# A two-part transformer kernel on one core: stacked attention scores, gathering that begins earlier, fewer chunks made ahead, and three changes of order

## The chip, the core and the metric

The kernel runs on one core of a Trainium2 chip. The metric is the device time of one execution in microseconds (us). TensorE does the matrix products, VectorE and ScalarE elementwise work, GpSimd and SyncE issue the transfers (GpSimd those that gather rows by index), and 16 DMA engines move the data. In the profile these are PE, DVE, ACT, POOL and SP; PEld is TensorE's loading of weights.

## The reference

All is float32, on 256 tokens of width 1024 and 256 context tokens. First come two layers of mix and PEER, then two layers of hybrid mixer and memory attention (not shown but for the hybrid's forget gates), then a norm.

```python
for l in range(2):                                   # first block
    f, p, q, k, v, gates = split_proj(h @ w_in[l])   # h: normed tokens; the context likewise
    q, k = rope(rmsnorm(q)), rope(rmsnorm(k))        # 8 query heads, 2 key heads of 64
    ya = attend(q, [k, k_ctx], [v, v_ctx]) @ attn_proj[l]     # 512 keys; context alone: 256
    x = x + gate * ((gates * [fourier(f), pool(p), ya]).sum() @ w_out[l])
    # PEER: 16384 experts, 8 heads, 16 experts per head and token
    q = (h2 @ wq).reshape(C, 8, 2, 128)
    s = einsum('chpd,hpnd->chpn', q, sub_keys)       # 128 keys in each of two halves
    s1, i1 = top_k(s[:, :, 0], 16); s2, i2 = top_k(s[:, :, 1], 16)
    top, pos = top_k(s1[..., None] + s2[..., None, :], 16)    # 16 of the 256 sums
    g = softmax(top)
    a = gelu(einsum('chkd,cd->chk', u_tab[eidx], h2))         # 128 experts per token
    x = x + gate * einsum('chk,chkd->cd', g * a, v_tab[eidx])
# second block, hybrid mixer: among its parts
log_f = log_sigmoid(f_b + b_forget)                  # forget gates, 8 heads
```

Layer 0 does PEER for tokens and context (512 rows), layer 1 for the 256 tokens alone.

## The kernel before

**Products in three passes.** A float32 product is made of a high and a low half: `split` writes the high half (L128, a cast on ScalarE, `whi` for weights) and the rest (L129, a subtraction on VectorE, `wlo`), and `mm3` makes three products of them (L186, L187, L188; at L824 a variant of it). Weights come through `wload` into five raw buffers and four split ones. A product with unsplit operands, such as that of L645, takes TensorE two records in the trace.

**Mix.** The projections, the attention units and the gates of a layer are woven together. `qk_unit` makes normed and rotated queries and keys and transposes them (L634) into `qT` and `kT`; `attn1_unit` makes the scores of two heads (L645), the softmax, its transposition (L652) and the product with `v` (L660). Layer 0 has eight such units on 512 keys and eight on 256 (the context), layer 1 eight on 512.

**PEER.** All 16384 experts lie in 128 chunks of 128. For a part of the tokens (the dense ones, 320 of 512 in layer 0 and 192 of 256 in layer 1) every chunk is computed: `expert_in` takes the chunk of `peer_uT` times the tokens and a gelu to `G`, `A` is `G` times a table of routing weights (`win`, read back from device memory, `wd`, eight chunks at a time, L788), is split to `Ahl`, and the `Ahl` products (L186 to L188 and L824) add the chunk of `peer_v` to sums kept in PSUM. The other 192 or 64 tokens are gathered (`gathered`): for each of them one transfer fetches the rows of its 128 experts from `peer_uv`, 8 KB each (`gat`, L893, four buffers); VectorE makes the dot products with them (L896) and adds the weighted second halves to `gacc` (L910). GpSimd issues the gathers, and each needs `idx`, which the last step of the routing writes (L993).

**What is made ahead.** While VectorE does the routing, TensorE makes the first chunks' `G`: `AHEAD`, 13 in layer 0 and 30 in layer 1. In layer 1 all 30 are whole (`WHOLE`, L851): unsplit weights, full-precision products; all others are split (three passes; at L859 and L860 in layer 1). The main loop over 128 chunks then starts. It makes a chunk's missing `G`, its `A` and `Ahl`, and asks for gathers by the rule quoted here, so that they are spread over the loop from chunk 5 on:

```python
while gat and done < min(max(c - 5, 0) * ng // 119, ng):
```

**Order.** The Tile framework's scheduler orders the instructions of each engine from the order of the code, the priorities and its own model; each engine runs its list in order. `ng` is the number of gathers, 192 or 64. In the hybrid, the forget gates (`wfd` weights, loaded and split on the spot, `fdT`, L1262) come first, before the gates and the conv units, whose weights are prefetched.

Of the kernel before, what the change touches and what calls it, by code (L numbers as in the profile page):

```python
# [35 lines left out]
AHEAD = 13, 30  # L36
WHOLE = 0, 30
# [11 lines left out]
class Net:  # L49
# [370 lines left out]
    def rope(self, out, src, cos, sin, nh, nb, f, pool):  # L420
# [11 lines left out]
        nc.vector.tensor_add(out, out, t[:, :w])  # L432
# [50 lines left out]
    def mix(self, l, both):  # L483
# [3 lines left out]
        with ExitStack() as es:  # L487
# [4 lines left out]
            oT = [ap.tile([128, 4, TB], FR, name=n) for n in ("oTh", "oTl")]  # L492
# [4 lines left out]
            qT = bp.tile([128, 4, TB], F32, name="qT")  # L497
            kT = self.k_padded(bp, "kT", T)
# [115 lines left out]
    def qk_unit(self, tp, rope, ps, t, gi, out, v):  # L614

        nc = self.nc
        cg, sg, kg = rope
        nh = 2 if gi else 8
        s = slice(t * 128, t * 128 + 128)
        q = self.headnorm(ps[:, :nh * 64], nh, tp)  # L620
        r = tp.tile([128, 512], F32, tag="qr", name="qr", bufs=3)[:, :nh * 64]
        if t < 2:
            self.rope(r, q, cg[:, gi, t], sg[:, gi, t], nh, 2, 16, tp)
        else:
            nc.vector.tensor_tensor(r3(r, nh), r3(q, nh), bc(kg[:, gi, None, :], [128, nh, 64]), op=OP.mult)
        if gi:
            self.evac(v[:, t], ps[:, 128:256])
        yield True
        if gi:
            self.k_put(out, r, tp, s)  # L630
            return
        pt = self.psum(True)
        for j in range(4):
            nc.tensor.transpose(pt[:, j * 128:(j + 1) * 128], r[:, j * 128:(j + 1) * 128], self.ident)  # L634
        self.evac(out[:, :, s], r3(pt, 4))

    def attn1_unit(self, tp, qT, kT, v, oT, st, j, qt):
# [6 lines left out]
        for hh in range(2):  # L644
            nc.tensor.matmul(ps[hh][:, :nk], qT[:, j, q0:q0 + 128], kT[:, hh, g, k0:k0 + nk], start=True, stop=True)  # L645
# [52 lines left out]
    def peer(self, l, both):  # L698
# [9 lines left out]
        with ExitStack() as es:  # L708
# [22 lines left out]
            with ExitStack() as e2:  # L731
                np_ = self.pool(e2, "wqp", side="right")
                scs, made = {}, []
                for cg in range(5):
                    qT = np_.tile([128, 4, 512], F32, tag="pq", name="pq", bufs=2) if cg < 4 else None
                    for c in range(4 if cg < 4 else 1):
                        if cg < 4:
                            ps = self.psum(c % 2)
                            self.proj_T(ps[:, :T], hT, i["wq"][l, cg * 4 + c], 0, T)
                            nc.scalar.copy(qT[:, c, :T], ps[:, :T])  # L740
                        if c == 0 and cg:
                            for t in range(NT):
                                ps = self.psum()
                                for k in range(4):
                                    nc.tensor.matmul(ps[:, k * 128:k * 128 + 128], pq[:, k, t * 128:t * 128 + 128], keys[:, k],
                                                     start=True, stop=True)
                                sc = scs[cg - 1, t] = np_.tile([128, 512], F32, tag="score", name="score", bufs=8)
                                nc.scalar.copy(sc, ps)
                    pq = qT
                    if cg < 4:  # L750
                        keys = np_.tile([128, 4, 128], F32, tag="keys", name="keys", bufs=2)
                        nc.gpsimd.dma_start(keys, i["keysT"][l, cg])
                    if cg:
                        for t in range(NT):
                            sc = scs[cg - 1, t]
                            for c in range(4):
                                n = (cg - 1) * 4 + c
                                self.top16(np_, sc[:, c * 128:c * 128 + 128], v16[t][:, n], i16[t][:, n], "tk")
# [915 lines left out]
```

## Time and profile before

| what | value |
|---|---|
| median of 3 runs | 3415.68 us (3409.3 to 3416.18) |
| profiled execution, its time | 3411.22 us |
| its span on the chip | 3409.4 us |
| TensorE, VectorE, ScalarE, GpSimd busy | 95%, 76%, 51%, 15% |
| mean granted clock of TensorE | 0.979 |
| moved by DMA | 860.52 MB, mean 252 GB/s |

The span is the time between the first and the last instruction of one execution; its own time is 1.8 us longer. The stages by time in the span: mix of layer 0 to 470 us, its PEER to 1740 (the routing ends near 784), mix of layer 1 to 1990, its PEER to 2757 (the routing ends near 2175), then the two layers of the second block to 3080 and 3409.4. Matrix products are pipelined: the distance from one start to the next, not a single duration, is what one costs. A granted clock of 1 is 2.4 GHz, 0.5 is 1.2 GHz.

### The profile page before, as it was taken

Reading aid. Unit: us, or ns where it says so; the run is one execution under the profiler, and the core shown is the slowest. Engines: PE = TensorE matmul, PEld = TensorE weight load, DVE = VectorE, ACT = ScalarE, POOL = GpSimd, SP = SyncE. Lnnn points to the kernel's source line nnn. Section 1 sums busy time; section 2 is a strip of 40 time slices with the busy share of each in tenths; the row PEclk is TensorE's granted clock in tenths of the full one; section 3 lists DMA queues with packets and bytes.
Section 4 is the critical chain, followed back from the end, with each engine's and each line's share of the span. In section 5 each row is a group of like instructions: output and inputs, shape, how many; then the busy total and the mean of one; then the engine's idle time right before and its main releaser. Section 6 shows DMA issues by size and latency. Waiting matters only on the chain.

```text
span 3409.4 us, 53017 instructions
## 1 busy us (share of the span) xinstructions
PE 3247.6 (95%) x19425; PEld 2779.9 (82%) x19425; DVE 2598.9 (76%) x5429; ACT 1734.0 (51%) x3711; POOL 515.9 (15%) x436
## 2 busy tenths in 40 slices
PE   8999999889999999999999998889999989999998
PEld 5666788768888888888877997769999989889887
DVE  3533449997989888999966678589999967755875
ACT  3443333385444444444444544557777745555554
POOL 0000000112333333333300000122222100000000
PEclk9999999889999999999999998999999999999999
DMA  6556232568999999999945555789999844255433
GB/s 244 193 194 219 88 128 80 173 177 312 377 398 379 378 381 372 379 392 389 390 158 173 166 178 170 267 340 389 372 370 377 346 159 161 93 189 174 142 120 109
DMA packets 196453, 860.52 MB, mean 252 GB/s; under 512 B 23920, under 2 KB 25664, under 8 KB 159712
## 3 DMA queue, kind: packets, MB, share of 16 engines
q1 hardware_dynamic: 141840, 505.94, 41.4%
q0 software_dynamic: 54352, 351.20, 26.8%
q8 instruction: 153, 2.51, 0.3%
q14 instruction: 108, 0.88, 0.1%
HBM read 816.15 MB, written 40.89 MB: 251 GB/s over the span
## 4 chain that ended last, share of the span: by engine, by line
PE 46%; issue 27%; DVE 12%; DMA 8%; POOL 6%; ACT 1%; POOLq 0%; DVEq 0%; SPq 0%; ACTq 0%
PE pf L188 5%; PE pf L186 5%; PE pf L187 5%; PE pf L860 4%; POOL gat L893 4%; PE ps L188 4%; PE ps L187 4%; PE ps L186 4%; DMA gat<-peer_uv,idx 4%; DVE wlo L129 3%; PE ps L824 3%; DVE gacc L910 2%; PE pf L859 2%; PE pf L370 1%; DMA wd<-wb 1%
## 5 line engine op out<-in xcount | busy, mean ns | idle before, releaser
L129 DVE TENSOR_TENSOR wlo<-raw,whi 128x1024 fp32r<-128x1024 f32 x778 | 940.1, 1219 | 388.2 <-ACT whi L128 378.2
L128 ACT CAST whi<-raw 128x1024 fp32r<-128x1024 f32 x778 | 814.4, 1047 | 572.8 <-PE pf L187 193.9
L893 POOL DMA_INDIRECT gat<-peer_uv,idx x256 | 406.2, 1587 | 917.3 <-DVE gacc L910 886.4
L188 PE MATMUL pf<-h2hl,wlo 128*128 128x320 f32 (+2 forms) x1152 | 368.6, 320 | 42.6 <-DVE wlo L129 42.5
L186 PE MATMUL pf<-h2hl,whi 128*128 128x320 f32 (+2 forms) x1152 | 367.2, 319 | 0.4 <-ACT mo L321 0.3
L187 PE MATMUL pf<-h2hl,whi 128*128 128x320 f32 (+2 forms) x1152 | 366.5, 318 | 0.0
L896 DVE SCALAR_TENSOR_TENSOR gat<-gat,h 128x1024 f32<-128x1024 f32 x256 | 311.5, 1217 | 70.2 <-DMA gat<-peer_uv,idx 69.8
L910 DVE SCALAR_TENSOR_TENSOR gacc<-gat,pga,gacc 128x1024 f32<-128x1024 f32 x253 | 322.9, 1276 | 0.0
L187 PE MATMUL ps<-wlo,Ahl 128*128 128x512 f32 x768 | 302.5, 394 | 6.2 <-DVE wlo L129 6.2
L186 PE MATMUL ps<-whi,Ahl 128*128 128x512 f32 x768 | 301.0, 396 | 4.1 <-ACT Ahl L128 4.1
L188 PE MATMUL ps<-whi,Ahl 128*128 128x512 f32 x768 | 301.6, 393 | 0.5 <-DVE Ahl L129 0.5
L188 PEld LDWEIGHTS pf<-h2hl,wlo 128*128 128x128 f32 x1152 | 221.9, 193 | 52.3 <-DVE wlo L129 49.6
L860 PE MATMUL pf<-h2hl,whi 128*128 128x384 f32 x784 | 238.5, 360 | 3.8 <-ACT whi L128 3.6
L186 PEld LDWEIGHTS pf<-h2hl,whi 128*128 128x128 f32 x1152 | 221.3, 192 | 8.1 <-ACT mo L321 0.5
L187 PEld LDWEIGHTS pf<-h2hl,whi 128*128 128x128 f32 x1152 | 221.4, 192 | 7.3
L128 ACT CAST Ahl<-A 128x320 fp32r<-128x320 f32 (+1 forms) x256 | 103.7, 405 | 218.1 <-DVE A L791 213.5
L859 PE MATMUL pf<-h2hl,wlo 128*128 128x192 f32 x686 | 174.9, 255 | 0.0
L188 PEld LDWEIGHTS ps<-whi,Ahl 128*128 128x128 f32 x768 | 145.0, 189 | 33.6 <-DVE Ahl L129 1.0
L187 PEld LDWEIGHTS ps<-wlo,Ahl 128*128 128x128 f32 x768 | 144.9, 189 | 31.0 <-DVE wlo L129 8.7
L186 PEld LDWEIGHTS ps<-whi,Ahl 128*128 128x128 f32 x768 | 144.9, 189 | 27.9 <-ACT Ahl L128 5.4
L897 ACT ACTIVATE pga<-pga 128x1 f32<-128x1 f32 x256 | 51.5, 201 | 226.1 <-DVE gat L896 225.7
L860 PEld LDWEIGHTS pf<-h2hl,whi 128*128 128x128 f32 x784 | 147.6, 188 | 8.6 <-ACT whi L128 4.4
(611 smaller groups left out, 7648.6 us busy)
## 6 DMA issues: line engine op xcount, KB each, us to landing
raw<-peer_uT SPq DMA_DIRECT2D x256, 512.0 KB
raw<-peer_v SPq DMA_DIRECT2D x256, 512.0 KB
raw<-ada_w SPq DMA_DIRECT2D x96, 512.0 KB
wd<-wb POOLq DMA_DIRECT2D x32, 1024.0 KB, 6.8
raw<-w_g SPq DMA_DIRECT2D x48, 512.0 KB
win<-wd POOLq DMA_DIRECT2D x16, 1280.0 KB, 9.5
raw<-wq SPq DMA_DIRECT2D x32, 512.0 KB
raw<-w2o SPq DMA_DIRECT2D x32, 512.0 KB
```

Source lines behind the costliest of these rows:

```text
L128: nc.scalar.copy(hi, src)
L129: nc.vector.tensor_sub(lo, src, hi.bitcast(F32))
L186: mm(ps, ah, bh, start=start, stop=False)
L187: mm(ps, ah, bl, start=False, stop=False)
L188: self.last = mm(ps, al, bh, start=False, stop=stop).ins
L824: nc.tensor.matmul(acc[nd][n], ahl[:, 2 * TD - part:], v[e][:, n], start=b == 0 and e == 0, stop=b == 127 and e == 1)
L859: mm(src, u[1][:, k], h2[:, k, 0, :TD], start=False, stop=False)
L860: self.last = mm(r3(ps[:, :2 * TD], 2), u[0][:, k], h2[:, k, :, :TD], start=k == 0, stop=k == 7).ins
L893: nc.gpsimd.indirect_dma_start(out=uv.rearrange("p a b -> p (a b)"), out_offset=None, in_=i["peer_uv"], in_offset=bass.IndirectOffsetOnAxi ...
L896: nc.vector.scalar_tensor_tensor(uv[:, 0], uv[:, 0], 1.0, h2, op0=OP.mult, op1=OP.mult, accum_out=a[:, 0:1])
L897: nc.scalar.activation(a[:, 1:2], a[:, 0:1], AF.Gelu_apprx_tanh)
L910: self.nc.vector.scalar_tensor_tensor(acc, uv[:, 1], a[:, 1:2], acc, op0=OP.mult, op1=OP.add)
```

## The change

Six edits are made together.

1. *Stacked scores.* Queries are written twice, one below the other: the high halves in rows 0 to 63 of `qT`, the low ones in rows 64 to 127; keys are written twice likewise and split to `kTh` and `kTl`. A score is then the sum of two single-pass products of 128 rows (L657). A query tile takes eight transposes instead of four.
2. *Softmax of routing.* It moves from ahead of the routing into it.
3. *Queries and scores.* The keys of the scores are loaded earlier, and in layer 1 the best-of-16 searches are emitted behind all scores instead of between them.
4. *Chunks ahead in layer 1.* 18 whole chunks instead of 30; the others are split in the main loop.
5. *Early gathering.* In layer 0 a gather is emitted after every second chunk made ahead, six in all; the rest are spread from chunk 2 to 124.
6. *Forget gates.* They become a unit that is joined with the third conv unit.

```diff
-AHEAD = 13, 30
-WHOLE = 0, 30
+AHEAD = 13, 18
+WHOLE = 0, 18
...
-            qT = bp.tile([128, 4, TB], F32, name="qT")
-            kT = self.k_padded(bp, "kT", T)
+            kT = [bp.tile([128, 2, T], FR, name=n) for n in ("kTh", "kTl")]
...
-        pt = self.psum(True)
-        for j in range(4):
-            nc.tensor.transpose(pt[:, j * 128:(j + 1) * 128], r[:, j * 128:(j + 1) * 128], self.ident)
-        self.evac(out[:, :, s], r3(pt, 4))
+        n = min(nh, 4)
+        for h0 in range(0, nh, n):
+            pt = self.psum(not gi)
+            for h in range(n):
+                nc.tensor.transpose(pt[:, h * 128:h * 128 + 128], r[:, h0 + h].rearrange("p a b -> p (a b)"), self.ident)
+            pt = r3(pt[:, :n * 128], n)
+            if gi:
+                self.split(pt, out[0][:, :, s], out[1][:, :, s])
+            else:
+                o = out[:, h0:h0 + n, s]
+                nc.scalar.copy(o, pt)
+                nc.vector.tensor_sub(o[64:128], pt[64:128], o[64:128].bitcast(F32))
...
-            nc.tensor.matmul(ps[hh][:, :nk], qT[:, j, q0:q0 + 128], kT[:, hh, g, k0:k0 + nk], start=True, stop=True)
+            for n, k in enumerate(kT):
+                nc.tensor.matmul(ps[hh][:, :nk], qT[:, 2 * j + hh, q0:q0 + 128], k[:, g, k0:k0 + nk], start=n == 0, stop=n == 1)
...
+                made = [scores(cg) for cg in range(4)]
                 for cg in range(5):
...
+                    if cg < 4:
+                        next(made[cg])
+                    if cg:
+                        for _ in made[cg - 1]:
+                            pass
+                    for _ in range(3 if cg < 4 else 0):
+                        next(made[cg])
+                    if cg and both:
+                        best(cg - 1)
+                if not both:
+                    for cg in range(4):
+                        best(cg)
...
-                for t in range(NT):
-                    self.soft(rp, top[t])
...
-            gs = [self.expert_in(lp, l, c, h2, h32, TD, c < WHOLE[l]) for c in range(ahead)]
             em.close()
+            gp = self.pool(es, f"gp{l}", side="right")
+            gat = self.gathered(gp, hT, idx, gg, TD, T) if ng else iter(())
+
+            gs, g0 = [], 0
+            for c in range(ahead):
+                gs.append(self.expert_in(lp, l, c, h2, h32, TD, c < WHOLE[l]))
+                if both and c % 2:
+                    next(gat, None)
+                    g0 += 1
...
-            done = 0
+            done, c0 = g0, 2
...
-                while gat and done < min(max(c - 5, 0) * ng // 119, ng):
+                while done < min(g0 + max(c - c0, 0) * (ng - g0) // (124 - c0), ng):
...
-        g = lp.tile([128, TD], F32, tag="G", name="G", bufs=15 if TD > 256 else 36)
+        g = lp.tile([128, TD], F32, tag="G", name="G", bufs=15 if TD > 256 else 22)
...
+        self.soft(rp, top)
         g = top.rearrange("p h s -> p (h s)")
...
                 gates = self.hybrid_gates(l, hT, gT)
-                self.weave((self.conv_unit(l, pp, hT, cw, m, xs, bcT) for m in range(12)), gates)
+                us = [self.conv_unit(l, pp, hT, cw, m, xs, bcT) for m in range(12)]
+                us[2] = self.joined(self.fd_unit(l, pp, hT, fd), us[2])
+                self.weave(us, gates)
...
+    def joined(a, b):
+
+        next(a, None)
+        yield from b
+        for _ in a:
+            pass
```

`scores` and `best` hold what stood in the loop before, and `fd_unit` holds the forget gates with a yield before their transposes. Three places in the engines' lists show what moves.

TensorE's list in the mix of layer 0, at the first attention unit, before (the L652 products transpose the softmax):

```order
L188 MATMUL pf<-frh,wlo 128x512
L370 MATMUL pf<-raw,cT 32x512 x6
L645 MATMUL ps<-kT,qT 128x512 x2
L652 MATMUL ps<-ident,p 128x128 x8
L186 MATMUL pf<-hTh,whi 128x512
```

The same place after the change:

```order
L188 MATMUL pf<-frh,wlo 128x512
L370 MATMUL pf<-raw,cT 32x512 x6
L657 MATMUL ps<-kTh,qT 128x512
L657 MATMUL ps<-kTl,qT 128x512
L657 MATMUL ps<-kTh,qT 128x512
L657 MATMUL ps<-kTl,qT 128x512
L664 MATMUL ps<-ident,p 128x128 x8
```

Two unsplit products became four single-pass ones; what stands around them is the same.

VectorE's list in layer 0, at the end of the routing, before (`pr` and `ef` are routing, `wlo` the splits of chunks made ahead and then of the main loop's weights):

```order
L972 SCALAR_TENSOR_TENSOR pr<-ab,ib 128x128 x29
L129 TENSOR_TENSOR wlo<-raw,whi 128x1024
L984 SCALAR_TENSOR_TENSOR ef<-ef 128x128
L129 TENSOR_TENSOR wlo<-raw,whi 128x1024
L993 CAST idx<-ef 128x128
L129 TENSOR_TENSOR wlo<-raw,whi 128x1024 x3
L791 TENSOR_TENSOR A<-G,win 128x320
L129 TENSOR_TENSOR wlo<-raw,whi 128x1024
L129 TENSOR_TENSOR Ahl<-A,Ahl 128x320
```

The same place after the change:

```order
L1004 SCALAR_TENSOR_TENSOR pr<-ab,ib 128x128 x31
L129 TENSOR_TENSOR wlo<-raw,whi 128x1024
L1017 SCALAR_TENSOR_TENSOR ef<-ef 128x128
L1026 CAST idx<-ef 128x128
L919 TENSOR_TENSOR hs<-h2hl 128x128 x8
L928 SCALAR_TENSOR_TENSOR gat,pga<-gat,h_7448 128x1024
L129 TENSOR_TENSOR wlo<-raw,whi 128x1024
L940 TENSOR_SCALAR gacc<-gat,pga 128x1024
L928 SCALAR_TENSOR_TENSOR gat,pga<-gat,h_7448 128x1024
L129 TENSOR_TENSOR wlo<-raw,whi 128x1024
L942 SCALAR_TENSOR_TENSOR gacc<-gat,pga,gacc 128x1024
```

The splits that followed `idx` now stand behind the work on gathered rows, one by one. TensorE has two chunks made ahead in front of the routing's last product instead of five and a part, and 264 products of L186 to L188 on `h2hl` behind it instead of 186.

TensorE's list in layer 1, at the end of the routing (L1028 is its last product), before:

```order
L1028 MATMUL ps<-o_21204,oh 128x128
L1028 LDWEIGHTS ol
L1028 MATMUL ps<-o_21204,ol 128x128
L851 MATMUL pf<-h2f,raw 128x192 x80
L186 MATMUL ps<-whi,Ahl 128x512
```

The same place after the change:

```order
L1061 MATMUL ps<-o_21278,oh 128x128
L1061 LDWEIGHTS ol
L1061 MATMUL ps<-o_21278,ol 128x128
L186 MATMUL ps<-whi,Ahl 128x512
L187 MATMUL ps<-wlo,Ahl 128x512
L188 MATMUL ps<-whi,Ahl 128x512
```

The ten whole chunks between the routing and the first chunk of the main loop are gone.

## Rows read from the trace of the kernel before

**Rows 1.** The page, part 1: busy us (share of the span) x instructions.

```profile
PE 3247.6 (95%) x19425; PEld 2779.9 (82%) x19425; DVE 2598.9 (76%) x5429; ACT 1734.0 (51%) x3711; POOL 515.9 (15%) x436
```

**Rows 2.** Windows, mix: length, PE, PEld, DVE, ACT, POOL busy, PEclk, DMA share, GB/s.

```profile
137.00:353.00 216.00, 214.31 (x1130) 133.55 (x1131) 84.54 (x206) 87.96 (x185) 0.00 (x0) 1.00 0.57 201
1845.00:1960.00 115.00, 115.00 (x950) 105.35 (x950) 73.78 (x136) 69.72 (x126) 0.00 (x0) 1.00 0.49 150
```

**Rows 3.** Windows, layer 0's PEER from the end of the routing on.

```profile
785.00:815.00 30.00, 29.99 (x191) 29.81 (x192) 16.20 (x22) 12.71 (x24) 5.25 (x6) 0.94 1.01 388
815.00:850.00 35.00, 35.00 (x158) 28.29 (x157) 29.87 (x47) 17.29 (x41) 9.70 (x7) 1.00 0.78 295
910.00:1700.00 790.00, 762.92 (x4186) 687.79 (x4185) 721.93 (x933) 376.53 (x860) 274.80 (x181) 0.99 0.98 384
```

**Rows 4.** Waits of TensorE, 850 to 1740: us in total, times, longest.

```profile
PE pf L188 <- DVE wlo L129: 33.7, 19, 4.1
```

**Rows 5.** Windows, layer 1's PEER from the end of the routing on.

```profile
2175.00:2205.00 30.00, 28.16 (x155) 27.59 (x155) 3.22 (x10) 5.49 (x20) 6.18 (x7) 0.89 0.89 334
2245.00:2295.00 50.00, 38.12 (x155) 28.95 (x155) 41.46 (x64) 23.84 (x57) 11.95 (x8) 0.93 0.87 333
```

**Rows 6.** Timeline of TensorE, attention: start us, us, engine, line, operation, count.

```profile
148.01 1.98 PE L645 MATMUL ps<-kT,qT 128*128 128x512 f32 x4
149.83 1.04 PE L652 MATMUL ps<-ident,p 128*128 128x128 f32 x8
...
301.42 1.13 PE L645 MATMUL ps<-kT,qT 128*128 128x256 f32 x4
302.49 0.66 PE L660 MATMUL ps<-pT,v 128*64 128x128 f32 x8
```

**Rows 7.** Timeline of TensorE, last chunk ahead and first `Ahl` products, layer 0.

```profile
812.76 0.31 PE L187 MATMUL pf<-h2hl,whi 128*128 128x320 f32 x1
...
813.93 0.40 PE L186 MATMUL ps<-whi,Ahl 128*128 128x512 f32 x1
...
814.87 0.39 PE L187 MATMUL ps<-wlo,Ahl 128*128 128x512 f32 x1
```

**Rows 8.** Timeline of TensorE, transposes of one query tile.

```profile
112.07 0.60 PE L634 MATMUL pf<-ident,qr 128*128 128x128 f32 x4
```

**Rows 9.** Timeline of VectorE, layer 0: `idx`, and the first `gat`.

```profile
786.21 0.22 DVE L993 CAST idx<-ef 128x128 int32<-128x128 f32 x1
...
828.31 1.22 DVE L896 SCALAR_TENSOR_TENSOR gat<-gat,h 128x1024 f32<-128x1024 f32 x1
```

**Rows 10.** Timeline of GpSimd, layer 0: gathers one, four and five.

```profile
789.32 1.02 POOL L893 DMA_INDIRECT gat<-peer_uv,idx  x1 [0.30 <-DMA raw<-peer_uT]
...
793.95 0.96 POOL L893 DMA_INDIRECT gat<-peer_uv,idx  x1 [0.30 <-issue]
...
833.17 1.69 POOL L893 DMA_INDIRECT gat<-peer_uv,idx  x1 [7.76 <-DVE gacc L908]
```

**Rows 11.** The tile `gat`, 780 to 860: from issue to landing.

```profile
DMA to landing us min/median/max: 8.0/10.5/12.9
```

**Rows 12.** Windows of L824 alone: length, PE and PEld busy (records), PEclk, DMA, GB/s.

```profile
910.00:1700.00 790.00, 113.60 (x420) 78.83 (x420) 0.99 0.98 384
...
2300.00:2700.00 400.00, 94.29 (x348) 65.35 (x348) 1.00 0.96 376
```

**Rows 13.** Timeline of TensorE, layer 1: whole chunks, then the first `Ahl` product.

```profile
2176.00 26.46 PE L851 MATMUL pf<-h2f,raw 128*128 128x192 f32 x144 [0.91 <-ACT G L869]
...
2205.94 0.53 PE L186 MATMUL ps<-whi,Ahl 128*128 128x512 f32 x1
```

**Rows 14.** Timeline of VectorE, layer 1: the first `A`, and its wait.

```profile
2187.96 0.63 DVE L791 TENSOR_TENSOR A<-G,win 128x192 f32<-128x192 f32 x2 [16.38 <-DMA win<-wd]
```

**Rows 15.** Windows, start of the first hybrid.

```profile
2776.00:2782.00 6.00, 5.82 (x28) 4.52 (x29) 1.58 (x2) 3.00 (x5) 0.00 (x0) 0.50 0.68 249
```

**Rows 16.** Waits of TensorE, 2740 to 2860: us in total, times, longest.

```profile
PE ps L186 <- ACT wfdh L128: 3.7, 1, 3.7
```

More of the change, by code (lines that the diff above doesn't have):

```diff
@@ L418, in headnorm, with rope @@
         return qn[:, :w]
-    def rope(self, out, src, cos, sin, nh, nb, f, pool):
+    def rope(self, out, src, cos, sin, nh, nb, f, pool, add=None):
         nc = self.nc
@@ L732, in peer @@
                 np_ = self.pool(e2, "wqp", side="right")
-                scs, made = {}, []
-                for cg in range(5):
[L735 to L741, printed above, removed]
-                            for t in range(NT):
[L743 to L749, printed above, removed]
+                scs = {}
@@ new lines, in scores @@
+                def scores(cg):
+                    qT = np_.tile([128, 4, 512], F32, tag="pq", name="pq", bufs=2)
+                    keys = np_.tile([128, 4, 128], F32, tag="keys", name="keys", bufs=2)
+                    nc.gpsimd.dma_start(keys, i["keysT"][l, cg])
+                    for c in range(4):
+                        ps = self.psum(c % 2)
+                        self.proj_T(ps[:, :T], hT, i["wq"][l, cg * 4 + c], 0, T)
+                        nc.scalar.copy(qT[:, c, :T], ps[:, :T])
+                        yield
+                    for t in range(NT):
+                        ps = self.psum()
+                        for k in range(4):
+                            nc.tensor.matmul(ps[:, k * 128:k * 128 + 128], qT[:, k, t * 128:t * 128 + 128], keys[:, k],
+                                             start=True, stop=True)
+                        sc = scs[cg, t] = np_.tile([128, 512], F32, tag="score", name="score", bufs=8)
+                        nc.scalar.copy(sc, ps)
@@ L750, in peer, with best @@
+                def best(cg):
+                    for t in range(NT):
+                        sc = scs[cg, t]
+                        for c in range(4):
+                            n = cg * 4 + c
+                            self.top16(np_, sc[:, c * 128:c * 128 + 128], v16[t][:, n], i16[t][:, n], "tk")
+                        self.candidates(np_, v16[t], top[t], pos[t], cg)
+                made = [scores(cg) for cg in range(4)]
+                for cg in range(5):
                     if cg < 4:
-                        keys = np_.tile([128, 4, 128], F32, tag="keys", name="keys", bufs=2)
@@ L802, in peer @@
                 if c == 125:
-                    for _ in gat or ():
+                    for _ in gat:
                         pass
```

60 lines of the change are left out of this document (28 added, 32 removed).

## The prediction

> **What bounds the kernel now.** The page comes first: TensorE is busy for 95% of the span, with 3247.6 of 3409.4 us [rows 1]; all that can go without taking work off it is 162 us. The windows by stage then say what a saving is worth where. In both attention stretches of the mix, TensorE runs 214.3 of 216 and 115.0 of 115 us [rows 2]: there a microsecond off TensorE is a microsecond off the end. In layer 0's expert loop TensorE has 762.9 of 790 us and the DMA engines are busy for 0.98 at 384 GB/s, VectorE for 722 us [rows 3]: three things stand close together, and the 27 us that TensorE lacks are waits on `wlo` (33.7 us from 850 to 1740) [rows 4]. In layer 1 the turn from the routing to the loop is the weak place: TensorE runs 38.1 of 50 us from 2245 on, and at a reduced clock from 2175 [rows 5].
>
> **Stacked scores.** The score products are full-precision today. One unit of two heads, 512 keys wide, holds TensorE from 148.01 until the next group at 149.83, 1.82 us for two products; a 256-wide unit from 301.42 to 302.49, 1.07 us [rows 6]. The new unit issues four single-pass products of 512 columns. Such products start 0.235 us apart (four from 813.93 to 814.87) [rows 7], so 0.94 us, and by half the width 0.47 us. There are 16 units at 512 (eight in each layer) and eight at 256 (layer 0's context): 16 x 0.88 + 8 x 0.60 = 18.9 us. Against it stand 24 more transposes (six query tiles, eight instead of four): four took 0.60 us [rows 8], so 3.6 us. The wider `qr` add, the copies of the hi half and the subtractions lie on VectorE and ScalarE, 85 and 88 us busy of 216 [rows 2]; uncovered they would cost TensorE a few us at the turn from the query stage. I take **+15** (bounds 10 and 18.9).
>
> **Early gathering, layer 0.** No gather or byte is added; gathers and products change places. First loss: inside the routing TensorE makes two of the 13 ahead chunks instead of 5.25, so 264 products stand behind the route's last one instead of 186; 78 x 0.147 us (eight from 812.76 to 813.93) = 11.5 us later start of the main loop [rows 7]. Second loss, from the order: VectorE's third ahead split is the last before `idx`; the fourth `wlo` now stands behind the first `gat`, which waits for its gather. `idx` is cast at 786.2, the first gather issues at 789.3 [rows 9, 10], and landing takes 8.0 to 12.9 us, median 10.5 [rows 11]. So that `wlo` is ready near 789.3 + 10.5 + 1.2 + 1.2 = 802. TensorE, done with the route near 784 and with `hs` transposes and one chunk (3.5 us) by about 790, waits about 12 us more, and the weights behind VectorE go on at 3.7 us a chunk (`wlo`, `gat`, `gacc`, each near the 1.22 us that a `gat` shows [rows 9]) instead of 3.5. The main loop thus starts about 24 us late, near 838 instead of 813.9.
>
> What it gains: before, four gathers are issued by 795 and the fifth at 833.2 [rows 10], while from 815 to 850 the DMA engines are busy for only 0.78 [rows 3]. After, about ten are through by then, and the rest go at 186 in 122 chunks (1.525 each) instead of 192 in 119 (1.613). A chunk needs 7.52 us now (420 records of L824, four a chunk, in 790 us) [rows 12]; TensorE's own work in it is 24 x 0.147 + 16 x 0.235 = 7.29 us. There are two ways to sum. By TensorE: -24 plus the part of the 33.7 us of waits that goes. By the DMA engines, since bytes are unchanged: the idle share 0.22 x 35 = 7.7 us before 850 is the gain, less what is left idle after. At 0.98 busy I go by the second, and take **+4**: TensorE's waits must then fall from 34 to about 6. Bounds: -24 (the stalls stay) and +22 (only the 11.5 us are lost and every wait goes).
>
> The DMA engines move 384 GB/s at 0.98 busy and 388 at 1.01 [rows 3], which I read as the limit. The Trainium skill's page "DMA: Bandwidth & Descriptors" (Specifications) puts a core's share of HBM at about 358 GB/s and the fabric's ceiling at 435; the trace already passes the first. By the second, 13% would be free, TensorE would be the bound, and the sum would be that of the first rival below.
>
> **18 instead of 30 chunks, layer 1.** After the route's last product TensorE now makes ten whole chunks, 2176.00 to 2205.94 [rows 13]. They go; 12 chunks more are split and made in the loop. A loop chunk takes 4.60 us (348 records, 87 chunks, 400 us) [rows 12]; its ten `Ahl` products are 2.35, so the split part is 2.25 and 12 of them 27.0 us. The main loop can't start at 2175: `A` waits for `win` until 2187.96 [rows 14], so its first product comes near 2189. TensorE stands idle for 14 us where it did 30 us of work. So far 30.8 - 14 - 27 = -10 us. What can come back is the 11.9 us of waits between 2245 and 2295 and some 3 us of reduced clock from 2175 to 2205 (0.89) [rows 5]: the `v` loads, gathers and windows get the idle 14 us for themselves. A half clock at the restart takes about 3 away (below). I take 12 back less 3: **-1**, bounds -14 (waits stay) and +5 (all go, no half clock).
>
> The 3 us are this row's: after a wait of 3.7 us in the first hybrid [rows 16] the granted clock was 0.50 from 2776 to 2782 [rows 15], the lower level of 1.2 GHz for 6 us, so 3 us of work lost. The Trainium skill's "TensorE: Matmul & The Clock Gate" (Part 1) says that the array goes to half rate after standing idle and comes back once it is busy; the trace agrees, 0.50 behind a wait. By that rule the ten whole chunks did cover work, and taking them out is charged twice, the idle time and the restart.
>
> **Forget gates.** The first hybrid now waits 3.7 us for `wfdh` [rows 16] and then runs 6 us at half clock [rows 15]. The joined unit comes behind conv products whose weights are prefetched, so both go: 3.7 + 3 = 6.7; some of the clock loss may stay. **+5** (bounds 0 and 6.7). The second hybrid has no such wait: 0.
>
> **The rest.** The softmax of routing moves behind the products, in front of the stage that needs it: VectorE has the same instructions, **-0.5**, bounds -1.5 and +1. The queries' order in layer 1 interleaves score products and best-of-16 search more finely; the instructions are the same in number and VectorE, not TensorE, sets the pace of that stretch: 0, bounds -2 and +2.
>
> **Sum.** 15 + 4 - 1 + 5 - 0.5 = 22.5 us off the profiled execution's 3411.2: 3388.7. That execution lies 4.5 us below the median of three, 3415.7, and inside their spread; **3389** is forecast.
>
> **Rivals.**
> *Layer 0's loop reaches TensorE's own rate.* If the first gather lands in 8 us and VectorE's thinner gathering removes every wait on `wlo`, the term is +22 instead of +4: 3371. For it: VectorE is 0.91 busy, and each gather costs it 2.5 us. Against: 0.98 busy DMA engines.
> *The late start is only half recovered.* Waits come in groups of eight chunks, with the `win` loads; if bursts cause them and not the mean load, 10 of 34 us go: -13, so 3406. For it: 19 waits, none over 4.1 us, and not a general slowness [rows 4].
> *No change that can be measured.* Nothing recovered: -24, which the other terms just balance: 3417.
> *Slower.* VectorE is in order, and six `gat` stand between the ahead splits. If gathers don't overlap there, each wait is 10.5 us: 63 us for splits that TensorE needs in 37, 26 us beyond the late start: -50 in layer 0, 3443. It decides once layer 0 loses more than about 30 us. Against: four buffers, and four issues within 5 us at 789 to 794 [rows 10].
> That the change does nothing where it says is excluded for the scores by the order, but it can be so for the gathering: the fourth rival.
>
> **How the numbers follow.** A measurement tells 0.2%, 6.8 us, from no change. The main case, 3376 to 3402, 0.60; the first rival, 3355 to 3376, 0.15; half recovered, 3402 to 3409, 0.11; no change, 0.09; slower, 0.05. Faster is 0.60 + 0.15 + 0.11 = 0.86. The range 3362 to 3409 leaves out about 0.06 below and 0.14 above.
>
> **What would show it.** Scores: two 512-wide units near 0.95 us each, and the first attention stretch about 9 us shorter. Layer 0: a first `Ahl` product near 838, TensorE idle around 790 to 802 with `wlo` as releaser, DMA busy for over 0.9 from 815 to 850, and under 15 us of waits on `wlo`. Layer 1: `Ahl` products 14 us behind the route's last product, a clock near 0.5 there, a stage about as long as before. Hybrid: no wait on `wfdh`. The forecast is wrong if the loop's waits stay near 34 us, or if the DMA engines show over 400 GB/s once the gathering starts early.

## The result, and the profile after

The changed kernel takes 3377.74 us (median of 4 runs, 3376.25 to 3379.98), the kernel before 3414.68 in the same comparison: a ratio of 0.9895, 95% interval 0.9878 to 0.9912, 36.9 us faster. 3389 was forecast, and the time lies inside the range. The profiled span fell from 3409.4 to 3377.0, by 32.4 us; the execution profiled before lies 3.5 us below that median. TensorE's line of the page, part 1, answers to [rows 1]: its work fell by 22 us and its idle time by 10.

```profile
PE 3225.6 (96%) x19449; PEld 2769.0 (82%) x19449; DVE 2623.5 (78%) x5454; ACT 1763.7 (52%) x3744; POOL 522.4 (15%) x432
```

Where the time went is read from the start times of five marks on TensorE: the first query product of a layer's PEER, the last product of its routing, its first and its last `Ahl` product (in layer 0 the last into `ps`; four into `pf` follow within 0.9 us, before and after), and the end. Some of the marks, in TensorE's timeline (start, duration, line, operation), of the kernel before beside [rows 7] and [rows 13]:

```profile
780.13 0.23 PE L1028 MATMUL ps<-o,ol 128*128 128x128 f16 x1
...
1745.76 0.39 PE L824 MATMUL ps<-wlo,Ahl 128*128 128x512 f32 x1
...
2174.81 0.29 PE L1028 MATMUL ps<-o,ol 128*128 128x128 f16 x1
```

The same marks of the changed kernel:

```profile
773.94 0.31 PE L1061 MATMUL ps<-o,ol 128*128 128x128 f16 x1
...
821.97 0.39 PE L186 MATMUL ps<-whi,Ahl 128*128 128x512 f32 x1
...
1719.54 0.40 PE L856 MATMUL ps<-wlo,Ahl 128*128 128x512 f32 x1
...
2157.45 0.79 PE L186 MATMUL ps<-whi,Ahl 128*128 128x512 f32 x1 [13.41 <-ACT Ahl L128]
```

The distances between the marks, in us of the two profiled executions:

| stretch | before | after | gain |
|---|---|---|---|
| start to layer 0's queries (mix) | 483.9 | 476.2 | 7.7 |
| queries to the routing's last product | 296.2 | 297.7 | -1.5 |
| routing to the first `Ahl` product | 33.8 | 48.0 | -14.2 |
| first to last `Ahl` product, layer 0 | 931.8 | 897.6 | 34.2 |
| to layer 1's queries (mix) | 251.6 | 246.8 | 4.8 |
| queries to the routing's last product | 177.4 | 177.5 | -0.1 |
| routing to the first `Ahl` product | 31.1 | 13.7 | 17.4 |
| first to last `Ahl` product, layer 1 | 543.6 | 563.5 | -19.9 |
| to the end (second block) | 659.8 | 656.1 | 3.7 |

**Scores.** TensorE's timeline of the changed kernel, one 512-wide unit and one 256-wide:

```profile
231.24 0.39 PE L657 MATMUL ps<-kTl,qT 128*128 128x512 f32 x1
231.47 0.40 PE L657 MATMUL ps<-kTh,qT 128*128 128x512 f32 x1
231.70 0.40 PE L657 MATMUL ps<-kTl,qT 128*128 128x512 f32 x1
...
257.94 0.28 PE L657 MATMUL ps<-kTl,qT 128*128 128x256 f32 x1
258.05 0.28 PE L657 MATMUL ps<-kTh,qT 128*128 128x256 f32 x1
```

The starts are 0.23 and 0.11 us apart, as forecast: four take 0.92 us where [rows 6] has 1.82, or 0.46 for 1.07.

**Layer 0.** Windows of the changed kernel (columns as in [rows 2]) answer to [rows 3]:

```profile
778.00:785.00 7.00, 5.12 (x21) 4.30 (x21) 3.41 (x11) 1.54 (x3) 3.08 (x4) 0.54 0.98 315
785.00:822.00 37.00, 37.00 (x255) 37.00 (x254) 33.22 (x44) 18.85 (x45) 12.84 (x10) 1.00 1.01 413
815.00:850.00 35.00, 35.00 (x170) 29.56 (x169) 33.59 (x44) 17.49 (x40) 11.69 (x10) 1.00 1.02 416
910.00:1700.00 790.00, 789.79 (x4372) 709.82 (x4372) 733.36 (x950) 399.04 (x878) 275.07 (x174) 1.00 0.98 383
```

Two things are to be seen. The loop's 27 us of idle TensorE are gone, 789.8 of 790 us, and yet the DMA row reads the same as before, 0.98 and 383 GB/s. And from 785 to 850, where the gathers now begin, the DMA engines move 413 to 416 GB/s. The waits of TensorE from 850 to 1740 answer to [rows 4]:

```profile
PE pf L188 <- DVE wlo L129: 7.1, 4, 3.1
PE ps L187 <- DVE wlo L129: 1.9, 1, 1.9
```

VectorE's wait for the landing of gathered rows fell with them, from the first line (before) to the second (changed kernel, both from 850 to 1740):

```profile
DVE gat L896 <- DMA gat<-peer_uv,idx: 69.8, 40, 6.1
...
DVE gat L928 <- DMA gat<-peer_uv,idx: 28.6, 20, 3.1
```

In the kernel before, the longest wait of TensorE on `wlo`, 4.1 us, stands behind the longest of these: VectorE waits 6.06 us for a landing, works on that gather and only then writes the `wlo` that TensorE waits for.

```profile
1322.23 1.23 DVE L896 SCALAR_TENSOR_TENSOR gat<-gat,h 128x1024 f32<-128x1024 f32 x1 [6.06 <-DMA gat<-peer_uv,idx]
...
1325.86 0.63 PE L188 MATMUL pf<-h2hl,wlo 128*128 128x320 f32 x1 [4.10 <-DVE wlo L129]
```

Behind that wait the products start 0.27 us apart instead of 0.147, at a granted clock of 0.50 from 1326 to 1330. Over the whole loop TensorE's idle time falls by 28 us (36.9 to 9.0); the other 6 of the 34.2 us lie in its busy time, at a lower clock behind the waits (mean 0.989 before, 0.998 after).

The stall of 12 us that was forecast for 790 to 802 isn't there. GpSimd's and VectorE's timelines of the changed kernel show why:

```profile
780.31 1.07 POOL L925 DMA_INDIRECT gat<-peer_uv,idx  x1 [3.86 <-PE pf L920]
```

```profile
786.94 1.23 DVE L928 SCALAR_TENSOR_TENSOR gat<-gat,h 128x1024 f32<-128x1024 f32 x1 [4.23 <-DMA gat<-peer_uv,idx]
```

The first gather issues 1.1 us behind the cast of `idx` (before, 3.1 us behind it) and is there 6.6 us later, not 10.5. In the kernel before, a window and the loads of `v` chunks were under way with it; that this made the difference is likely, but was not tried.

**Layer 1.** TensorE waits for `Ahl` for 13.4 us behind the routing (the last row of the marks above, 14 forecast), at the lower clock, and the clock is still at 0.50 for the first 5 us of the loop:

```profile
2143.00:2158.00 15.00, 1.58 (x8) 0.88 (x8) 1.09 (x4) 2.57 (x9) 5.96 (x7) 0.50 0.71 220
2158.00:2163.00 5.00, 5.00 (x14) 3.83 (x13) 2.96 (x11) 2.30 (x7) 0.26 (x1) 0.50 0.98 395
```

**Hybrid.** Of the waits of [rows 16] (2720 to 2860 here) the one on `wfdh` is gone; a smaller one has come:

```profile
PE ps L262 <- DVE dg L249: 3.7, 1, 3.7
PE ps L1220 <- ACT cacc L1216: 1.6, 1, 1.6
```

### The profile page after: what moved, and what is told of

It is laid out like the page before. It is cut to its first block, busy times and chain, and to the rows that moved or that the text cites. A ratio compares the mean times of both kernels' runs of the same rounds, so it can differ in the third digit from the quotient of the medians.

```text
span 3377.0 us, 53113 instructions
## 1 busy us (share of the span) xinstructions
PE 3225.6 (96%) x19449; PEld 2769.0 (82%) x19449; DVE 2623.5 (78%) x5454; ACT 1763.7 (52%) x3744; POOL 522.4 (15%) x432
## 4 chain that ended last, share of the span: by engine, by line
PE 69%; issue 17%; DVE 5%; DMA 5%; ACT 2%; POOL 2%; SPq 0%; POOLq 0%; DVEq 0%; ACTq 0%
PE pf L188 8%; PE pf L186 8%; PE pf L187 8%; PE ps L187 7%; PE ps L186 7%; PE ps L188 7%; PE pf L892 5%; PE ps L856 5%; PE pf L891 2%; PE pf L370 2%; PE pf L856 1%; DVE wlo L129 1%; DMA wd<-wb 1%; PE ps L262 1%; DMA gat<-peer_uv,idx 1%
## 5 line engine op out<-in xcount | busy, mean ns | idle before, releaser
L129 DVE TENSOR_TENSOR wlo<-raw,whi 128x1024 fp32r<-128x1024 f32 x790 | 958.2, 1222 | 382.7 <-ACT whi L128 371.8
L128 ACT CAST whi<-raw 128x1024 fp32r<-128x1024 f32 x790 | 827.7, 1048 | 612.6 <-PE pf L187 231.3
L925 POOL DMA_INDIRECT gat<-peer_uv,idx x256 | 416.3, 1626 | 943.6 <-DVE gacc L942 896.8
L188 PE MATMUL pf<-h2hl,wlo 128*128 128x320 f32 (+2 forms) x1152 | 361.6, 314 | 10.2 <-DVE wlo L129 10.2
L186 PE MATMUL pf<-h2hl,whi 128*128 128x320 f32 (+2 forms) x1152 | 362.4, 315 | 0.2 <-ACT mo L321 0.2
L187 PE MATMUL pf<-h2hl,whi 128*128 128x320 f32 (+2 forms) x1152 | 361.7, 314 | 0.0
L928 DVE SCALAR_TENSOR_TENSOR gat<-gat,h 128x1024 f32<-128x1024 f32 x256 | 312.3, 1220 | 35.6 <-DMA gat<-peer_uv,idx 34.2
L186 PE MATMUL ps<-whi,Ahl 128*128 128x512 f32 x768 | 302.9, 397 | 15.8 <-ACT Ahl L128 15.8
L187 PE MATMUL ps<-wlo,Ahl 128*128 128x512 f32 x768 | 304.9, 397 | 4.7 <-DVE wlo L129 4.6
L188 PE MATMUL ps<-whi,Ahl 128*128 128x512 f32 x768 | 302.8, 394 | 0.6 <-DVE Ahl L129 0.6
L892 PE MATMUL pf<-h2hl,whi 128*128 128x384 f32 x880 | 267.3, 359 | 2.5 <-ACT whi L128 2.3
L188 PEld LDWEIGHTS pf<-h2hl,wlo 128*128 128x128 f32 x1152 | 217.9, 189 | 14.5 <-DVE wlo L129 11.7
L187 PEld LDWEIGHTS pf<-h2hl,whi 128*128 128x128 f32 x1152 | 217.9, 189 | 7.9
L186 PEld LDWEIGHTS pf<-h2hl,whi 128*128 128x128 f32 x1152 | 217.9, 189 | 7.8 <-ACT mo L321 0.3
L891 PE MATMUL pf<-h2hl,wlo 128*128 128x192 f32 x770 | 196.3, 255 | 0.0
L186 PEld LDWEIGHTS ps<-whi,Ahl 128*128 128x128 f32 x768 | 145.0, 189 | 40.9 <-ACT Ahl L128 16.8
L188 PEld LDWEIGHTS ps<-whi,Ahl 128*128 128x128 f32 x768 | 144.6, 188 | 34.8 <-DVE Ahl L129 1.0
L892 PEld LDWEIGHTS pf<-h2hl,whi 128*128 128x128 f32 x880 | 165.6, 188 | 7.4 <-ACT whi L128 2.7
L856 PE MATMUL ps<-wlo,Ahl 128*128 128x512 f32 x384 | 152.2, 397 | 0.0
```

Source lines behind the costliest of these rows:

```text
L128: nc.scalar.copy(hi, src)
L129: nc.vector.tensor_sub(lo, src, hi.bitcast(F32))
L186: mm(ps, ah, bh, start=start, stop=False)
L187: mm(ps, ah, bl, start=False, stop=False)
L188: self.last = mm(ps, al, bh, start=False, stop=stop).ins
L856: nc.tensor.matmul(acc[nd][n], ahl[:, 2 * TD - part:], v[e][:, n], start=b == 0 and e == 0, stop=b == 127 and e == 1)
```

## The experiments

All start from the changed kernel unless said otherwise. Times are medians against the kernel before on the same chip; the distances of the table above, from each run's own profile, tell small edits apart better than the times, whose single runs spread over 4 to 17 us in one kernel. The 0.2% of the forecast is the size of such an interval.

**No early gathering** (`a1_no_early`).

```diff
-                if both and c % 2:
-                    next(gat, None)
-                    g0 += 1
...
-            done, c0 = g0, 2
+            done, c0 = g0, 5
```

> The changed kernel without early gathering (no gather during the chunks made ahead; the rest by the old rule, 192 gathers over 119 chunks from chunk 5). Theory 1 (layer 0's gain comes from the early gathering): the first Ahl product comes 34 us behind the routing's last product instead of 48, but the loop from the first to the last Ahl product takes 932 us again instead of 898, with over 25 us of TensorE waits on wlo from 850 to 1740 instead of 7. Time 3378 + 34 - 14 = 3398 us, ratio to the kernel before 0.995. Rival (the loop's gain comes from another of the edits, or from chance): the loop stays below 910 us, and the time falls to 3378 - 14 + 10 = 3374 us or less.

Measured: 3392.41 us, ratio 0.9941 (0.9922 to 0.996). The first `Ahl` product comes 33.9 us behind the routing, the loop takes 932.0 us, and the waits are back (TensorE, 850 to 1740):

```profile
PE pf L188 <- DVE wlo L129: 31.1, 19, 3.1
```

Its windows show the idle DMA time of before again, and the loop:

```profile
815.00:850.00 35.00, 32.71 (x148) 26.22 (x147) 30.37 (x49) 16.82 (x40) 11.24 (x8) 1.00 0.81 300
910.00:1700.00 790.00, 766.48 (x4201) 691.70 (x4200) 722.43 (x934) 378.84 (x865) 274.40 (x181) 0.99 0.98 384
```

So the whole of layer 0's change, the late start and the shorter loop, is the early gathering. The time is 6 us under the 3398 of theory 1, since the same edit let layer 1 gather from chunk 5 (556.9 us for 563.5, below).

**Thinner gathering without the six ahead** (`b2_thin_only`). Only the three lines of the `if` are taken out; `c0` stays 2.

> The changed kernel without the six gathers during the chunks made ahead, but with gathering from chunk 2 on, 192 over 122 chunks (1.574 a chunk; before 1.613, after 1.525). Theory 1a (what counts is how many gathers fall on a chunk, in proportion): half of the loop's 34 us come back, the loop takes about 915 us, and the main loop starts 14 us earlier than in the changed kernel: 3378 + 17 - 14 = 3381 us. Theory 1b (what counts is a lead of gathers made in idle time of the DMA engines): the loop takes about 930 us, 3396 us. Theory 1c (the old rate lies just above what VectorE and the DMA engines can follow, the new one below): the loop takes 900 us, 3366 us, faster than the changed kernel.

Measured: 3387.17 us (3376.89 to 3394.07), ratio 0.9928 (0.9907 to 0.9949); start 34.1 us behind the routing, loop 914.1 us, waits on `wlo`:

```profile
PE pf L188 <- DVE wlo L129: 12.1, 9, 2.9
PE ps L187 <- DVE wlo L129: 4.0, 1, 4.0
```

This is theory 1a: the loop's length follows the gathers that fall on a chunk, 932 at 1.613, 914 at 1.574, 898 at 1.525. By the start times the 14 us saved at the front and the 16.5 lost in the loop nearly balance; the median is 9 us above the changed kernel's, in runs that spread over 17. Start and loop together take 948.2 us here, 965.6 before and 945.6 in the changed kernel; four runs below with layer 0's gathering unchanged lie between 946.3 and 950.7. So most of layer 0's gain, 17 of 20 us, comes with the thinner rate alone, and that the six gathers ahead add to it isn't shown.

**Six gathers ahead, old rate behind them** (`b3_lead_only`).

```diff
-            done, c0 = g0, 2
+            done, c0 = g0, 9
```

> The changed kernel with its six gathers during the chunks made ahead, but the other 186 only from chunk 9 on, over 115 chunks (1.617 a chunk, as before the change), so that the lead of six is used up by chunk 16. Theory 1a and 1c (gathers per chunk): the loop takes 925 to 932 us again, with waits on wlo over 25 us, and the late start stays: 3378 + 30 = 3408 us. Theory 1b (six gathers moved into idle time): the loop stays at 900 us, 3380 us.

Measured: 3399.04 us, ratio 0.9952 (0.9937 to 0.9968); start 49.1 us, loop 927.8 us, and TensorE's waits 27.6 us in 16 places:

```profile
PE pf L188 <- DVE wlo L129: 27.6, 16, 4.1
```

A lead of six that is used up by chunk 16 gives 4 of the 34 us. Theory 1b (the lead) falls. The total came out at 3399 where 3408 was expected, since layer 1's loop gained by the same edit (below).

**One product of three left out** (`c1_two_passes`): the expert chunk's product in layer 0 lacks the weights' low half, and `wload` doesn't make that half (not shown); 860.4 MB are moved, 860.5 in the changed kernel.

```diff
-                    self.mm3(src, (u[0][:, k], u[1][:, k]), (h2[:, k, 0, :TD], h2[:, k, 1, :TD]), k == 0, k == 7)
+                    mm(src, u[0][:, k], h2[:, k, 0, :TD], start=k == 0, stop=False)
+                    mm(src, u[0][:, k], h2[:, k, 1, :TD], start=False, stop=k == 7)
```

> The changed kernel with the first product of an expert chunk in layer 0 made in two passes instead of three: the product with the weights' low half is left out, and with it the split's subtraction on VectorE; bytes are the same. TensorE's work per chunk falls from 7.25 to 6.07 us, VectorE's from 6.7 to 5.5; a chunk moves 2.81 MB. Theory D1 (the DMA engines are full at 384 GB/s, as the prediction took it): a chunk stays at 7.2 to 7.3 us, and the loop at 890 to 900 us. Theory D2 (their limit is higher, 410 to 425 GB/s as in the stretch from 785 to 850): a chunk takes 6.6 to 6.85 us, the loop 820 to 850 us. Theory D3 (no limit there): 6.1 us, 760 us.

Measured: 3333.09 us in one run, loop 863.6 us, 6.75 a chunk. That is D2's time a chunk (6.6 to 6.85), while the loop is 14 us above what D2 said for it; D1 and D3 fall. The window of its loop:

```profile
910.00:1600.00 690.00, 631.95 (x3197) 543.77 (x3198) 566.41 (x773) 357.03 (x809) 229.18 (x167) 0.98 1.01 411
```

TensorE and VectorE have 58 and 124 us to spare, and the DMA engines move 411 GB/s at a busy share of 1.01, so 384 wasn't their limit. VectorE waits, 850 to 1680, for gathered rows:

```profile
DVE gat L933 <- DMA gat<-peer_uv,idx: 134.5, 109, 5.5
```

So this loop is held up by the transfers. Whether by the rate of the engines or by the time that one gather takes to land, with four buffers, wasn't tried.

**Plain scores** (`a2_plain_scores`): the scores, queries and keys of before; of the edit, the scores.

```diff
-            for n, k in enumerate(kT):
-                nc.tensor.matmul(ps[hh][:, :nk], qT[:, 2 * j + hh, q0:q0 + 128], k[:, g, k0:k0 + nk], start=n == 0, stop=n == 1)
+            nc.tensor.matmul(ps[hh][:, :nk], qT[:, j, q0:q0 + 128], kT[:, hh, g, k0:k0 + nk], start=True, stop=True)
```

> The changed kernel with the scores of before (one full-precision product each, four transposes a query tile, keys padded). Theory S1 (the prediction's: two single-pass products for one full-precision one, minus the transposes): the mix of layer 0 ends 7 to 9 us later (first product of the queries at 484 instead of 476.2), that of layer 1 5 to 6 us later, the time is 3378 + 13 = 3391 us. Rival S2 (a part of the mix's 12.6 us came from the order of other work there): the mixes lose under 8 us together, 3386 us or less.

Measured: 3391.49 us, ratio 0.9935 (0.9914 to 0.9956). Layer 0's queries begin at 487.6, layer 1's mix takes 249.0: 11.4 and 2.2 us, together 13.6 where S1 had 13, shared otherwise between the layers than expected. Over the runs with stacked scores the first mark lies between 474.1 and 478.6, so 2 us either way is the spread of an execution.

**30 whole chunks** (`a3_whole30`).

```diff
-AHEAD = 13, 18
-WHOLE = 0, 18
+AHEAD = 13, 30
+WHOLE = 0, 30
```

> The changed kernel with 30 whole chunks ahead in layer 1, as before. Theory W1 (cutting to 18 cost a little, as the milestones say: 17 us earlier start, 20 us longer loop): the main loop of layer 1 starts 31 us behind the routing instead of 14 and takes 544 us instead of 563: 3378 - 2 = 3375 us. Rival W2 (the cut gains, and what costs 3 to 7 us in layer 1 is its gathering from chunk 2 instead of 5, which the runs without the early rule show as a loop of 557 us): the loop with 30 chunks takes 548 to 552 us, and the time is 3380 to 3383 us.

Measured: 3374.30 us, ratio 0.9889 (0.9869 to 0.9909). Start 27.8 us behind the routing, loop 547.9: together 575.7 where 18 chunks have 577.2, and from 574.2 to 576.1 in five more runs with 18 chunks and the same gathering in layer 1. The loop is at the edge of what W2 said (548 to 552) and the time is W1's: how many chunks are made ahead makes no difference that can be told here.

**Layer 1's gathers from chunk 5** (`f1_l1_from5`).

```diff
-            done, c0 = g0, 2
+            done, c0 = g0, 2 if both else 5
```

> The changed kernel with layer 1's gathers spread from chunk 5 on as before (64 over 119), layer 0 as changed. Theory W2 (the earlier start in layer 1 falls into the stretch in which the loop runs on Ahl products alone and needs the most data, and costs 4 to 6 us): the loop of layer 1 takes 557 us instead of 561 to 563, 3373 us. Rival (the 557 us of the two runs that had this rule come from their other state, not from the rule): 561 to 563 us, 3378 us.

Measured: 3374.24 us, ratio 0.9879 (0.9864 to 0.9894); layer 1's loop takes 557.3 us for 563.5. The two runs that had this rule by the way show 556.9 (from 5) and 556.5 (from 9), and the six with chunk 2 and 18 chunks, the changed kernel among them, 560.6 to 563.5. So the earlier start in layer 1 costs 3 to 7 us, which all edits carry that share the one `c0`.

**Forget gates first** (`a4_fd_first`): the unit stands ahead of the conv units again.

> The changed kernel with the forget gates first again in the hybrid. Theory F1: TensorE waits 3.7 us for wfdh once more and runs at half clock for some us, the part behind layer 1's loop takes 660 us instead of 656, the time is 3378 + 4 = 3382 us. Rival F2 (the wait was there but the time behind it is given back by later waits): 3378 us, with the wait in the trace.

Measured: 3382.02 us (3373.78 to 3387.34), ratio 0.9901 (0.9878 to 0.9925): the time alone decides nothing. The second block takes 659.2 us, 3.1 more than in the changed kernel (654.0 to 657.6 in all the runs with the joined unit), and the wait is there (2690 to 2860):

```profile
PE ps L186 <- ACT wfdh L128: 3.7, 1, 3.7
```

**Gathers after ahead chunks 5 to 12** (`d1_gather_from5`).

```diff
-                if both and c % 2:
+                if both and c >= 5:
```

> The changed kernel with its first gathers one after each of the ahead chunks 5 to 12 (eight instead of six), so that TensorE's list has 190 products behind the routing's last one as in the kernel before (186), not 264. Theory G1 (the late start comes from the place of the first gather in the order, and the loop's gain from 1.51 to 1.53 gathers a chunk): the first Ahl product comes 35 us behind the routing instead of 48, the loop stays at 898 us: 3378 - 13 = 3365 us. Rival G2 (the 11 chunks at 785 to 822 were what let the gathers run ahead; with a shorter stage the loop meets them in waits): the loop takes 910 us, 3377 us.

Measured: 3382.71 us, ratio 0.9914 (0.9893 to 0.9936). The start came 47.2 us behind the routing all the same, loop 902.8 (897.6 to 902.4 in the runs with layer 0's gathering unchanged): neither G1's 35 nor G2's 910. GpSimd's timeline shows a cause: the first window stands behind eight gathers, which wait for the four buffers.

```profile
789.08 1.26 POOL L925 DMA_INDIRECT gat<-peer_uv,idx  x1 [0.30 <-issue]
796.10 0.93 POOL L925 DMA_INDIRECT gat<-peer_uv,idx  x1 [5.76 <-DVE gacc L940]
...
808.92 1.67 POOL L925 DMA_INDIRECT gat<-peer_uv,idx  x1 [3.18 <-DVE gacc L942]
810.58 0.62 POOL L820 DMA_DIRECT2D win<-wd  x1
```

**Windows first, 18, 24 and 30 whole chunks** (`e1_win_first_18`, `e2_win_first_24`, `e3_win_first_30`). To the edit above come two windows asked for ahead of the gathers, and layer 1 gathers from chunk 5:

```diff
+            def load(c):
+                win = gp.tile([128, TD // 16, 8, 16], F32, tag="win", name="win", bufs=2)
+                return win, nc.gpsimd.dma_start(win.rearrange("p b c t -> p (b c t)"), wd[c // 8])
+
+            wins = {c: load(c) for c in range(0, 8 * 2, 8)} if both else {}
...
```

> The first gathers come after ahead chunks 5 to 12, the first two windows of layer 0 are asked for ahead of them on GpSimd's queue, and layer 1 gathers from chunk 5; 18 whole chunks. Theory G3 (in the run with gathers from chunk 5 the late start stayed because the first window stood behind eight gathers in GpSimd's queue): the first Ahl product comes 34 to 36 us behind the routing instead of 47, the loop of layer 0 takes 900 to 905 us, that of layer 1 557: 3378 - 13 + 5 - 5 = 3365 us. Rival G2 (time won at the start is lost again in the first 16 chunks, where gathers, windows and weights compete for the DMA engines): the loop of layer 0 takes 912 us or more, 3373 us.

> As the run with 18 chunks of this call, with 24 whole chunks ahead in layer 1. If start and loop trade evenly (18 chunks: 14 and 557 us; 30 chunks before the change: 31 and 544), the sum stays at 571 to 575 us for any number, and the time is that of the run with 18 within 3 us. Rival (24 fill TensorE's idle 14 us at no cost): the loop starts 16 us behind the routing and takes 550 us, 5 us less.

> As the run with 18 chunks of this call, with 30 whole chunks ahead in layer 1. Theory W1/W2: the loop of layer 1 starts 28 to 31 us behind the routing and takes 543 us, 571 to 574 in all, the same as with 18 within 3 us: 3365 us. If the cut to 18 was worth its place, this run is 4 us slower or more.

Measured: 3384.68 us (0.9908, 0.9892 to 0.9924), 3377.42 (0.9893, 0.988 to 0.9906) and 3375.47 (0.9883, 0.9869 to 0.9897). Layer 0 starts 37.9, 40.3 and 37.9 us behind the routing, near the 34 to 36 of G3, and its loop takes 917.1, 915.2 and 916.6 us, as G2 said. So the window behind the gathers was indeed what kept the start late. All three times lie over the 3365 to 3373 us expected, and 9 us apart where 3 were expected. The windows of the run with 18 show where the loop loses:

```profile
815.00:850.00 35.00, 28.38 (x114) 22.23 (x112) 31.05 (x38) 14.69 (x36) 13.43 (x10) 0.90 0.98 378
850.00:910.00 60.00, 51.50 (x233) 42.30 (x234) 56.70 (x76) 24.11 (x61) 21.73 (x16) 0.89 0.97 383
...
1000.00:1700.00 700.00, 700.00 (x3870) 629.19 (x3869) 640.96 (x828) 353.23 (x775) 244.51 (x155) 1.00 0.98 383
```

TensorE idles 15 us in the first two, at a clock of 0.90 and 0.89, with VectorE busy for 31 of 35 and 56.7 of 60 us: the work on gathered rows meets the loop's first chunks instead of the chunks made ahead, which need only half of a chunk's weights. Start and loop together take 955.0 us where the changed kernel takes 945.6. The late start was thus not a loss to be taken away by this edit; that it is the room in which the gathers run is how the windows read; no run shows it by itself.

From 1000 us on, TensorE doesn't idle at all. There the rule of gathers on a chunk holds in every run with all products: from 1000 to 1700 TensorE idles 21.2 to 25.6 us at 1.613 to 1.617 a chunk, 11.3 us at 1.574, 0.2 to 2.4 at the changed kernel's 1.525 and 0.0 with eight gathers ahead (1.508). Ahead of 1000 us it doesn't hold: the three runs with windows first gather at 1.508 too, and their loops are 18 to 20 us longer than the changed kernel's.

In layer 1, start and loop together take 570.9, 571.2 and 568.4 us with 18, 24 and 30 whole chunks: the number hardly matters, and by the last of the three expectations the cut to 18 wasn't worth its place. No version is told apart from the changed kernel as faster: the lowest, with layer 1 gathering from chunk 5, has 0.9864 to 0.9894 against 0.9878 to 0.9912.

## Why the time lay in the predicted range, and which terms were off

**Stacked scores: +15, measured 12.5** (7.7 and 4.8; 13.6 when the edit is undone). The mechanism and the price of a product are shown. The term is 2.5 us too large, which lies within the spread of the marks; TensorE waits 1.8 us for the new subtractions of the queries, a cost that the prediction named but left out of its +15.

**Early gathering: +4, measured 20.0** (34.2 less 14.2). This is the step that failed. The prediction had two sums, and chose the DMA engines' because of 0.98 busy at 384 GB/s. The changed kernel shows the same 0.98 and 383 GB/s with TensorE at full work, and the run with a product left out shows 411: the rate was what the loop asked for, not what the engines could give. By the prediction's own sign this step was wrong: it named over 400 GB/s once the gathering starts early, and 413 to 416 came. The trace of the kernel before had shown it already, in a stretch where TensorE hardly idles:

```profile
1550.00:1600.00 50.00, 49.02 (x274) 44.35 (x273) 45.43 (x60) 24.11 (x57) 18.07 (x12) 1.00 1.00 403
```

The sum by TensorE was the right one, with both of its parts mis-sized. The late start was 14.2 us, not 24: the 78 products of 11.5 us, 1.9 us of waits on `hs`, and some of the clock's fall to 0.54 from 778 to 785; the wait behind the first `gat` was nearly nothing, since the gather landed in 6.6 us. The loop's gain was 34.2 us with 9 us of waits left, since a wait costs clock behind it too, some 6 us in all, which the sum put at nothing. So in this layer the first rival came true, near its price of +22, while the whole stayed in the main case's range, 3376 to 3402, at its lower end. The Trainium skill's 435 GB/s ("DMA: Bandwidth & Descriptors", Specifications) stood behind that rival: the highest over 30 us in any run is 420 (`a3_whole30`, 802 to 832), and none holds 435.

What freed the loop, past its first 100 us or so, is the number of gathers on a chunk; the run with six gathers ahead but the old rate excludes the lead as such. How a thinner rate frees it is read from traces, not shown by a run. VectorE's splits stand behind `gat` in its order, and a `gat` waits for its landing: of the 20 waits on `wlo` from 850 us on in the kernel before, 18, with 28 of 34 us, come within 12 us behind waits of VectorE for landings that together last at least 0.8 times as long. Each gather less on a chunk takes 2.5 us from VectorE too; how much that part weighs stays open.

**18 whole chunks: -1, measured -2.5** (17.4 less 19.9). Start and half clock came as worked out: 13.4 us of waiting, 0.50 behind it. The Trainium skill's rule of half rate after standing idle ("TensorE: Matmul & The Clock Gate", Part 1) agrees with this row as well. But that -1 and -2.5 lie close is luck, for three things make up the -2.5, and two of them the prediction priced nowhere or at nothing. From 574.7 us before, start and loop together fall to 568.4 in the run with 30 whole chunks and gathering from chunk 5, both as before: 6.3 us come from the other edits. About half of them can be one whole chunk of 3 us that no longer stands behind the routing (144 records of whole chunks against 160); the rest stays open. The cut to 18 then costs 2.5 us (570.9), about as much as marks differ between executions. Layer 1's gathering from chunk 2 costs the remaining 6.3 (577.2; 6.2 in the loop of its own run). The same rule that helps layer 0 hurts here; the loop's first 15 chunks or so are `Ahl` products alone and come fastest, and an earlier gather falls among them; that this is why it costs is argued, not shown.

**Forget gates: +5, measured 3.7** (3.1 when undone): the wait of 3.7 us on `wfdh` went, but a new one of 1.6 us on `cacc` came, which the forecast had not.

**The rest: -0.5, measured -1.5 and -0.1** on the two stretches from queries to routing's end. Neither differs from the spread: in the changed kernel and four runs that change nothing up to there, layer 0's stretch lies between 297.4 and 302.6 us.

Sum: 12.5 + 20.0 - 2.5 + 3.7 - 1.6 = 32.1 us of the 32.4 between the spans, where 22.5 were forecast. Early gathering gave 16 us more than its term and the others together 6.4 less: that the time lay in a range of 47 us is in part luck. The other rivals, half recovered (by its own terms -24 + 10 = -14, not -13), no change and slower, ask for TensorE's waits to stay at 24 us or more or for gathers that don't overlap; the waits are 9 us, and the four first gathers issue within 5 us.

## What to carry to other kernels

A busy share of the DMA engines near 1 with an unchanged rate doesn't prove that they are the limit: look for a stretch of the same loop with a higher rate, or take work off the compute engines, as in the run with a product left out, and see whether the rate rises. When several streams share a loop, spread the one that has slack over all of the time in which it could run; here, past the loop's first 100 us, the mean number of gathers on a chunk decided, not the lead of the first ones. And before shortening a stage that looks late, ask what runs in its shadow: in the runs with windows first, layer 0's main loop started 8 to 10 us earlier and took 18 to 20 us longer, with the waits in its first chunks.

## What the runs showed of the hardware that had not been expected

The DMA engines of one core moved 411 GB/s over 690 us (413 to 416 in the changed kernel over 35 to 37) with a mix of 8 KB gathered rows and direct loads, at busy shares of 1.01 to 1.02, while 383 GB/s already reads as 0.98. A wait of 4.1 us was followed by products at half clock, 0.27 us apart instead of 0.147, for 5 us: of the 34 us that layer 0's loop gained, some 6 are such lost clock. And the stretch of layer 0's scores and routing took 297.4 to 302.6 us in profiled executions of kernels that don't differ up to there; its cause wasn't looked for.
